# Gate/up blocks 2 to 9 of both FFNs by 7 products of halves instead of blocks 2, 3, 5, 6 and 7, with 3 of the 7 second weight parts made by adding transfers

## The chip, the core and the metric

One core of a Trainium2 chip runs the whole program. The metric is the device time of one execution in microseconds, the median of several runs.

## The reference, cut to what matters

A decoder layer on 512 rows of 1024 numbers: an FFN, a token mixer, a second FFN, each between norms. The change is in the two FFNs, which compute, with `w_gu` of 1024 x 5632 and `w_dn` of 2816 x 1024:

```python
def swiglu(h, w_gu, w_dn):
    g, u = jnp.split(h @ w_gu, 2, axis=-1)
    return (jax.nn.silu(g) * u) @ w_dn
...
        h = rmsnorm(x, g_pre[l, 0]) * (1 + sc1) + sh1
        x = x + 0.5 * gt1 * rmsnorm(swiglu(h, w_gu1[l], w_dn1[l]), g_post[l, 0])
```

Everything is float32 in and out.

## The kernel before

**Precision.** A float32 operand is used as two parts: `hi`, the value rounded for the matrix engine (made by ScalarE, ACT), and `lo`, the rest (made by VectorE, DVE, as the value minus `hi`). A product of two float32 tiles is three matmuls (`hi hi`, `hi lo`, `lo hi`), all accumulated in PSUM. `split` makes the two parts of a weight tile of 128 x 1024 numbers. Its outputs are called `whi` and `wlo`, and each of the two has `NW = 5` buffers; a weight as it comes from memory is called `raw`, and there are `NRAW = 4` buffers for it, 512 KB each.

**Gate/up.** The columns of `w_gu` are worked off in 11 blocks of 256 gate and 256 up columns. A plain block loads four `raw` tiles, splits them and runs 96 matmuls with 512 columns (four accumulators, 8 rows of tiles, 3 matmuls each; line 381). The blocks in `SEVEN` go through the function `seven` instead: the four `raw` tiles are taken as the four quarters a11, a12 (gate columns, upper and lower half of the contraction), a21, a22 (up columns) of a 2 x 2 matrix of blocks, and the output comes from 7 products of halves instead of 8. Seven weight combinations are needed: l11 = a11, l12 = a12, l22 = a22 as they are, and l1, l2, l3, l4, which are sums and differences, made by DVE in place in the `raw` tiles (4 instructions, lines 413 to 421). Each of the seven is split (7 ACT and 7 DVE instructions, lines 156 and 157), and each is the left side of 24 matmuls with 256 columns (line 429), in the order l11, l2, l1, l3, l12, l22, l4. Between the products DVE adds the partial results (`plus`, line 435, 5 instructions); the last of these, `gate2`, needs the whole block. Then ACT and DVE form silu(g) * u and split it for the down projection (lines 455 to 460).

**Order.** The instructions of each engine are in a fixed order, which a scheduler has laid down when the program was built; each engine works its own list off in order and waits at semaphores. SP issues the loads, also in a fixed order; a load waits until its buffer is free.

**Down projection.** `down` runs over two halves of the output columns (`dh`), and in each over 11 pairs of rows of `w_dn` (24 matmuls of 512 columns for a pair, line 193). In the first FFN, four pieces of the conditioning for the mixer (`mod_cols`: 2 MB of `w_ada`, 8 DVE multiply-adds, 8 small matmuls, line 269) are worked in beside plain gate/up blocks, at blocks 4, 8, 9 and 10. The residual rows (`xt`, 8 tiles) stay in SBUF through the FFN.

Of the kernel before, what the change touches and what calls it, by code (L numbers as in the profile page):

```python
# [8 lines left out]
F32 = mybir.dt.float32  # L9
F32R = mybir.dt.float32r  # L10
U8 = mybir.dt.uint8
BF16 = mybir.dt.bfloat16
AF = mybir.ActivationFunctionType
ALU = mybir.AluOpType

P = 128
T = 512
# [13 lines left out]
NW = 5  # L31
NMM = 6
LOOK = 4
SEVEN = (2, 3, 5, 6, 7)
KTAIL = 6
ROWS_A = (4, 5, 5, 4)

# [3 lines left out]
def tile_hybrid_layer(  # L41
# [17 lines left out]
    def nm(s):  # L59
        uid[0] += 1  # L60
        return f"{s}_{uid[0]}"
# [10 lines left out]
    def acc(shape=(P, 512)):  # L72
        return pm.tile(list(shape), F32, tag="mm", name=nm("mm"))
# [49 lines left out]
    def load_x(src, pin, between=()):  # L123
        for t in range(NT):
            xt[t] = [unit(), unit()]
            for h in range(2):
                i = nc.sync.dma_start(xt[t][h], src[t * P:(t + 1) * P, h * 512:(h + 1) * 512])
                if pin:
                    tc.keep_in_program_order(i)
                if between:  # L130
                    nc.sync.dma_start(*between.pop(0))
# [16 lines left out]
    def raw_load(src, shape):  # L148
        raw = sb.tile([P] + list(shape), F32, tag="raw", bufs=NRAW, name=nm("raw"))
        nc.sync.dma_start(raw, src)  # L150
        return raw

    def split(raw, shape, eng=None):
        hi = sb.tile([P] + list(shape), F32R, tag="whi", bufs=NW, name=nm("whi"))
        lo = sb.tile([P] + list(shape), F32R, tag="wlo", bufs=NW, name=nm("wlo"))
        nc.scalar.copy(hi, raw)  # L156
        (eng or nc.vector).tensor_tensor(lo, raw, hi.bitcast(F32), ALU.subtract)  # L157
        return hi, lo
# [32 lines left out]
    def mm3(ps, a, b, first, last):  # L191
        for n, (i, j) in enumerate(PARTS):
            nc.tensor.matmul(ps, a[i], b[j], start=first and n == 0, stop=last and n == 2)  # L193

    def cut(pair, cs):
        return pair[0][:, cs], pair[1][:, cs]
# [205 lines left out]
    def seven(w_gu, jb, hs, rs, act):  # L402

        gw, uw = gu_blocks(w_gu, jb)
        for b in (gw, uw):
            b.fetch()
        a11, a12, a21, a22 = gw.raw[0], gw.raw[4], uw.raw[0], uw.raw[4]
        t1, t2, t3, t4 = rs
        b11, b21, b22 = [lambda k, e, k0=k0, ts=ts: hs[k0 + k][e][:, ts] for k0, ts in
                         ((0, slice(0, 256)), (4, slice(0, 256)), (4, slice(256, 512)))]  # L410
        sh = (4, 256)
        l11 = split(a11, sh)
        nc.vector.tensor_tensor(a21, a21, a22, ALU.add)  # L413
        l1 = split(a21, sh)
        nc.vector.tensor_tensor(a21, a21, a11, ALU.subtract)
        l2 = split(a21, sh)
        l22 = split(a22, sh)
        nc.vector.tensor_tensor(a22, a22, a21, ALU.subtract)
        l3 = split(a22, sh)
        l12 = split(a12, sh)  # L420
        nc.vector.tensor_tensor(a12, a12, a21, ALU.subtract)
        l4 = split(a12, sh)
        x, y, z = [acc((P, 2, 256)) for _ in range(3)]

        def product(ps, left, right, first=False):
            for k in range(4):
                for j in range(2):
                    for n, (i, e) in enumerate(PARTS):
                        nc.tensor.matmul(ps[:, j], left[i][:, k, j * P:(j + 1) * P], right(k, e),  # L429
                                         start=first and k + j + n == 0, stop=k == 3 and n == 2,  # L430
                                         skip_group_check=True)

        def plus(ps, a, out=None):
            o = tmp((P, 2, 256)) if out is None else out
            nc.vector.tensor_tensor(o, ps, a, ALU.add)
            return o

        product(x, l11, b11, True)
        p1 = tmp((P, 2, 256))
        nc.scalar.copy(p1, x)  # L440
        product(y, l2, t2, True)
        u2 = plus(y, p1)
        product(z, l1, t1, True)
        product(y, l3, t3)
        u3 = plus(y, p1)
        up2 = plus(z, u3, u3)
        product(x, l12, b21)
        product(y, l22, t4)
        product(z, l4, b22)
        up1 = plus(y, p1, p1)  # L450
        gate2 = plus(z, u2, u2)
        a = [(unit(F32R), unit(F32R)) for _ in range(2)]
        for h, (g, u) in enumerate(((x, up1), (gate2, up2))):
            th = tmp((P, 2, 256))
            nc.scalar.activation(th, g, AF.Tanh, scale=0.5)
            nc.vector.scalar_tensor_tensor(th, th, 1.0, g, ALU.add, ALU.mult)
            nc.vector.scalar_tensor_tensor(th, th, 0.5, u, ALU.mult, ALU.mult)
            for j in range(2):
                ts = slice(h * 256, (h + 1) * 256)
                hilo(a[j][0][:, ts], a[j][1][:, ts], th[:, j])  # L460
        act.extend(a)

    def ffn(w_gu, w_dn, hs, extra, gate, after, ps=None, by_seven=(), keep=None):

        act = []
        rest = [b for b in range(KF // 2) if b not in by_seven][-len(extra):] if extra else []
        for jb in range(KF // 2):
            if by_seven and jb == 1:
                rs = right_sides(keep)
            if jb in by_seven:  # L470
                seven(w_gu, jb, hs, rs, act)
                continue
            if ps is None:
                gw, uw = gu_blocks(w_gu, jb)
                for kk in range(0, KD, 4):
                    gw.load(kk, kk + 4)
                    uw.load(kk, kk + 4)
                late = extra.pop(0)() if jb in rest else None
                ps = [[acc(), acc()] for _ in range(2)]
                for ts in (slice(0, 256), slice(256, 512)) if jb == 0 else (slice(0, 512),):  # L480
                    for kk in range(0, KD, 4):
                        gu_matmuls(ps, gw, uw, hs, range(kk, kk + 4), ts)
                if late:
                    late()
            for pg, pu in ps:
                th = tmp()
                nc.scalar.activation(th, pg, AF.Tanh, scale=0.5)
                nc.vector.scalar_tensor_tensor(th, th, 1.0, pg, ALU.add, ALU.mult)
                nc.vector.scalar_tensor_tensor(th, th, 0.5, pu, ALU.mult, ALU.mult)  # L489
                a = (unit(F32R), unit(F32R))  # L490
                hilo(a[0], a[1], th)
                act.append(a)
            ps = None
        down(w_dn, act, gate, after)

    def down(w, act, gate, after):
        nk = len(act)
        ss = [small(2, "ss", 4) for _ in range(NT)]
        yg = None
        g = []  # L500
        for dh in range(2):
            ys = [acc() for _ in range(NT)]
            groups = [(k, 2) for k in range(0, nk, 2)]
            if dh == 1:
                groups = groups[:-KTAIL // 2] + [(nk - KTAIL, KTAIL)]
            for k0, n in groups:
                wp = Block(w, k0, n, dh * 512, 512)
                wp.load()
                if dh == 0 and k0 in (0, 4):
                    gate(g, k0 // 4)  # L510
                for t in range(NT):
                    ts = slice(t * P, (t + 1) * P)
                    for k in range(n):
                        mm3(ys[t], cut(act[k0 + k], ts), wp[k], k0 + k == 0, k0 + k == nk - 1)
            if dh == 0:
                yg = [unit() for _ in range(NT)]
                post_first(ys, g[0], ss, yg)
            else:
                for t in range(NT):
                    post_second(t, ys[t], g[1], ss, yg)  # L520
                    after(t)
# [87 lines left out]

    with not_before(last):  # L610
        ffn(w_gu1[0], w_dn1[0], hs, extra, lambda g, h: mod_gate(g, 0, h, 0.5), after1, ps0, SEVEN,
            (1, lambda tp, k: xT[k][:, tp * 256:(tp + 1) * 256].unsqueeze(1)))
    hs = nxt[-1]


# [586 lines left out]
    load_x(xd, True)  # L1202

    h3 = {}

    def after2(t):
        if t == 0:
            nxt.append(h_tiles())
        if t % 2:
            make_h(t // 2, nxt[-1], sh3, sc3, h3)  # L1210

    down(w_out, mrg, lambda g, h: mod_gate(g, 1, h, 1.0), after2)


    def after3(t):
# [1 line left out]
            nc.sync.dma_start(out[t * P:(t + 1) * P, h * 512:(h + 1) * 512], xt[t][h])  # L1217

    ffn(w_gu2[0], w_dn2[0], nxt[-1], [], lambda g, h: mod_gate(g, 2, h, 0.5), after3,
        by_seven=SEVEN, keep=(2, lambda tp, k: h3[tp, k // 2]))  # L1220


# [26 lines left out]
```

## Time and profile before

| | |
|---|---|
| median of 3 runs | 1432.32 us (1431.89 to 1432.74) |
| the profiled execution | 1435.03 us, span in the profile 1433.3 us |
| PE (matmul) busy | 1375.0 us, 96% |
| DVE busy | 896.1 us, 63% |
| ACT busy | 577.7 us, 40% |
| POOL busy | 206.7 us, 14% |
| mean granted TensorE clock | 0.996 |

The profile is of one execution. PE is TensorE, DVE VectorE, ACT ScalarE, POOL GpSimd, and SP the engine that issues the loads; busy time is the union of an engine's instructions, and the span runs from the first to the last instruction. Stretches are given in us from the span's start. In the first FFN the gate/up blocks 2 to 10 run from 89.8 to 287 us and the down projection to 405 us; in the second FFN they run from 1108.4 to 1300.8 us, with the down projection behind them up to the end.

### The profile page before, as it was taken

The numbers are of one execution on the slowest core, as the hardware profiler recorded it, in microseconds if no ns is written. First come the engines' busy times: TensorE is split into PE (matmuls) and PEld (weight loads), VectorE is DVE, ScalarE is ACT, GpSimd is POOL, SyncE is SP. The second block draws the span as 40 slices with busy tenths as digits, with TensorE's granted clock in tenths as the row PEclk, the third lists the DMA queues.
The fourth block names the chain that finished last, engine by engine and source line by source line (L and its number), as shares of the span: only waits on it lengthen the run. The fifth ranks groups of instructions, "written<-read, shape, count | busy, mean of one in ns | idle before, by whom it ended". The sixth has DMA issues, their size and how long they took to land.

```text
span 1433.3 us, 18789 instructions
## 1 busy us (share of the span) xinstructions
PE 1375.0 (96%) x7197; PEld 1141.6 (80%) x7197; DVE 896.1 (63%) x1398; ACT 577.7 (40%) x999; POOL 206.7 (14%) x328
## 2 busy tenths in 40 slices
PE   4899999999999999999999999999999999999998
PEld 3699998878877877777888887788878989887886
DVE  6889797562266689762735546538577878637222
ACT  6444453232144476663723333333344434423221
POOL 5300000000051553440110202100050000000001
PEclk9999999999999999999999999999999999999999
DMA  9425237473235756322232232124611332436311
GB/s 323 141 67 165 86 111 226 146 243 98 88 121 165 232 156 176 90 67 88 88 111 81 59 87 61 59 74 140 228 59 60 103 105 87 147 88 196 127 59 59
DMA packets 160629, 174.49 MB, mean 122 GB/s; under 512 B 8842, under 2 KB 127734, under 8 KB 160540
## 3 DMA queue, kind: packets, MB, share of 16 engines
q1 hardware_dynamic: 160540, 173.31, 39.2%
q8 instruction: 56, 0.92, 0.3%
q14 instruction: 33, 0.27, 0.1%
HBM read 169.05 MB, written 4.23 MB: 121 GB/s over the span
## 4 chain that ended last, share of the span: by engine, by line
PE 73%; DVE 14%; DMA 4%; ACT 4%; issue 3%; POOL 1%; SPq 0%; DVEq 0%; ACTq 0%; POOLq 0%
PE mm L193 46%; PE mm L381 15%; PE mm L429 6%; DVE wlo L157 3%; ACT whi L156 2%; DMA raw<-in_w_gu_dram 2%; PE aux L1069 1%; DMA u<-in_w_ada_dram 1%; DVE u L200 1%; PE aux L880 1%; DVE u L868 1%; PE mm L891 1%; DVE t L214 1%; ACT u L864 1%; DVE raw L413 1%
## 5 line engine op out<-in xcount | busy, mean ns | idle before, releaser
L157 DVE TENSOR_TENSOR wlo<-raw,whi 128x1024 fp32r<-128x1024 f32 x248 | 307.9, 1249 | 293.0 <-ACT whi L156 284.0
L156 ACT CAST whi<-raw 128x1024 fp32r<-128x1024 f32 x250 | 259.5, 1050 | 482.1 <-PE mm L193 297.0
L193 PE MATMUL mm<-whi,u 128*128 128x512 f32 x1216 | 390.2, 397 | 1.5 <-ACT u L199 1.5
L193 PE MATMUL mm<-u,whi 128*128 128x512 f32 x896 | 289.5, 402 | 0.8 <-DVE u L1096 0.8
L193 PEld LDWEIGHTS mm<-whi,u 128*128 128x128 f32 x1216 | 228.2, 188 | 54.3 <-ACT u L199 1.7
L381 PE MATMUL mm<-u,whi 128*128 128x512 f32 (+1 forms) x832 | 249.6, 385 | 10.8 <-ACT u L199 9.7
L193 PE MATMUL mm<-wlo,u 128*128 128x512 f32 x608 | 240.4, 395 | 0.0
L429 PE MATMUL mm<-u,whi 128*128 128x256 f32 x1120 | 200.0, 281 | 2.4 <-ACT whi L156 2.1
L193 PEld LDWEIGHTS mm<-u,whi 128*128 128x128 f32 x896 | 167.0, 189 | 39.2 <-DVE u L1096 1.2
L381 PEld LDWEIGHTS mm<-u,whi 128*128 128x128 f32 x832 | 153.6, 190 | 46.5 <-ACT u L199 13.0
L193 PE MATMUL mm<-u,wlo 128*128 128x512 f32 x448 | 178.4, 399 | 0.0
L429 PEld LDWEIGHTS mm<-u,whi 128*128 128x128 f32 x1120 | 171.7, 188 | 4.0 <-ACT whi L156 3.2
L429 PE MATMUL mm<-u,wlo 128*128 128x256 f32 x560 | 157.1, 282 | 2.2 <-DVE wlo L157 2.2
L381 PE MATMUL mm<-u,wlo 128*128 128x512 f32 (+1 forms) x416 | 156.1, 382 | 0.0
L193 PEld LDWEIGHTS mm<-wlo,u 128*128 128x128 f32 x608 | 114.2, 188 | 27.8
L429 PEld LDWEIGHTS mm<-u,wlo 128*128 128x128 f32 x560 | 105.2, 188 | 3.3 <-DVE wlo L157 3.0
L193 PEld LDWEIGHTS mm<-u,wlo 128*128 128x128 f32 x448 | 84.7, 189 | 19.6
L308 POOL TENSOR_SCALAR sm<-ss 128x1 f32<-128x1 f32 x12 | 2.3, 192 | 651.4 <-ACT jk L315 651.4
L381 PEld LDWEIGHTS mm<-u,wlo 128*128 128x128 f32 x416 | 79.3, 191 | 16.2
L214 DVE SCALAR_TENSOR_TENSOR t<-raw,csil,t 128x512 f32<-128x512 f32 x98 | 74.2, 757 | 3.5 <-DMA raw<-in_w_ada_dram 1.4
L199 ACT CAST u<-t 128x256 fp32r<-128x256 f32 (+1 forms) x80 | 36.0, 469 | 75.5 <-DVE t L489 47.7
L837 POOL TENSOR_SCALAR u<-t,Ft 128x128 f32<-128x128 f32 (+1 forms) x64 | 41.9, 665 | 91.5 <-DMA t<-Fd 61.7
(201 smaller groups left out, 1384.8 us busy)
## 6 DMA issues: line engine op xcount, KB each, us to landing
raw<-in_w_gu_dram SPq DMA_DIRECT2D x88, 512.0 KB, 3.5
raw<-in_w_in_dram SPq DMA_DIRECT2D x64, 512.0 KB, 3.8
raw<-in_w_dn_dram SPq DMA_DIRECT2D x44, 512.0 KB, 3.9
raw<-in_w_ada_dram SPq DMA_DIRECT2D x64, 256.0 KB, 3.8
raw<-in_w_ada_dram SPq DMA_DIRECT2D x24, 512.0 KB, 4.7
u<-in_w_ada_dram SPq DMA_DIRECT2D x32, 256.0 KB, 6.4
raw<-in_w_in_dram SPq DMA_DIRECT2D x20, 256.0 KB, 2.9
t<-Fd SPq DMA_DIRECT2D x16, 256.0 KB, 5.1
```

Of the source, the lines that this page charges most:

```text
L156: nc.scalar.copy(hi, raw)
L157: (eng or nc.vector).tensor_tensor(lo, raw, hi.bitcast(F32), ALU.subtract)
L193: nc.tensor.matmul(ps, a[i], b[j], start=first and n == 0, stop=last and n == 2)
L199: nc.scalar.copy(hi, src)
L200: (eng or nc.vector).tensor_tensor(lo, src, hi.bitcast(F32), ALU.subtract)
L214: nc.vector.scalar_tensor_tensor(a, raw[:, j, :], csil[:, k:k + 1], a, ALU.mult, ALU.add)
L381: nc.tensor.matmul(p_[:, ts], w_[k][i][:, cs], hs[k][e][:, ts], start=ks[0] == 0 and n == 0, stop=ks[-1] == KD - 1 and n == 3 * len(ks) - 1)
L413: nc.vector.tensor_tensor(a21, a21, a22, ALU.add)
L429: nc.tensor.matmul(ps[:, j], left[i][:, k, j * P:(j + 1) * P], right(k, e), start=first and k + j + n == 0, stop=k == 3 and n == 2, skip_g ...
L837: nc.gpsimd.tensor_scalar(s_at(s, i), fb[:, 0:n], -1.0, Ft[:, i, h:h + 1], ALU.mult, ALU.add)
L864: nc.scalar.activation(s_at(S[e], i), s_at(S[e], i), AF.Exp, bias=nmx[e][:, i:i + 1], accum_out=rs[e][:, i:i + 1])
L868: nc.vector.tensor_scalar(s_at(S[e], i), s_at(S[e], i), rs[e][:, i:i + 1], None, ALU.mult)
```

## The change

`SEVEN` becomes all blocks from 2 to 9. In `seven` the combinations are made in another order and stand in other tiles, and three of the seven (l12, l22 and l4) are no longer split by DVE: ACT writes `hi` and then also the negative of the value, rounded, to `wlo`, and a transfer that POOL issues adds the value to it in place. The four pieces of the conditioning move: one to block 10, three into the first half of the down projection. The residual rows are no longer held through the FFN: they are loaded again (in the first FFN from the input, in the second from a copy `xe` in memory that is stored behind the mixer) at the start of the second half of the down projection.

```diff
-SEVEN = (2, 3, 5, 6, 7)
+SEVEN = tuple(range(2, 10))
...
+    def split_added(raw, shape):
+
+        hi = sb.tile([P] + list(shape), F32R, tag="whi", bufs=NW, name=nm("whi"))
+        lo = sb.tile([P] + list(shape), F32R, tag="wlo", bufs=NW, name=nm("wlo"))
+        nc.scalar.copy(hi, raw)
+        nc.scalar.activation(lo, raw, AF.Copy, scale=-1.0)
+        nc.gpsimd.dma_start(lo.bitcast(F32), raw, accum_op=ALU.add)
+        return hi, lo
...
+        nc.vector.tensor_tensor(a21, a21, a22, ALU.add)
         l11 = split(a11, sh)
-        nc.vector.tensor_tensor(a21, a21, a22, ALU.add)
+        nc.vector.tensor_tensor(a11, a21, a11, ALU.subtract)
+        l2 = split(a11, sh)
         l1 = split(a21, sh)
-        nc.vector.tensor_tensor(a21, a21, a11, ALU.subtract)
-        l2 = split(a21, sh)
-        l22 = split(a22, sh)
-        nc.vector.tensor_tensor(a22, a22, a21, ALU.subtract)
-        l3 = split(a22, sh)
-        l12 = split(a12, sh)
-        nc.vector.tensor_tensor(a12, a12, a21, ALU.subtract)
-        l4 = split(a12, sh)
+        nc.vector.tensor_tensor(a21, a22, a11, ALU.subtract)
+        l3 = split(a21, sh)
+        l12 = split_added(a12, sh)
+        l22 = split_added(a22, sh)
+        nc.vector.tensor_tensor(a11, a12, a11, ALU.subtract)
+        l4 = split_added(a11, sh)
...
-                late = extra.pop(0)() if jb in rest else None
+                late = extra.pop(0)() if extra and jb == KF // 2 - 1 else None
...
+            if dh == 1 and source is not None:
+                load_x(source, True)
...
+                late = extra.pop(0)() if extra and dh == 0 and k0 > 4 and k0 % 4 == 0 else None
...
+        for h in range(2):
+            nc.sync.dma_start(xe[t * P:(t + 1) * P, h * 512:(h + 1) * 512], xt[t][h])
```

Three places in the engines' lists show what the change makes of the order. All are of the first FFN, from block 6 to block 7; the second FFN reads alike.

The first is DVE at the end of block 6, before the change. `mm_317` and `mm_318` are accumulators of block 6, `raw_328` to `raw_331` are the tiles a11, a12, a21, a22 of block 7. L435 with `mm_318` at the sixth row is `gate2` of block 6, L415 makes l2 of block 7, and the last row is the second part of l2.

```order
L456 SCALAR_TENSOR_TENSOR t2_326_1889<-t2_326_1889,mm_316_1705 128x512
L413 TENSOR_TENSOR raw_330_1909<-raw_330_1909,raw_331_1911 128x1024
L435 TENSOR_TENSOR t2_319_1732<-mm_317_1706,t2_319_1732 128x512
L457 SCALAR_TENSOR_TENSOR t2_326_1889<-t2_326_1889,t2_319_1732 128x512
L157 TENSOR_TENSOR wlo_335_1919<-raw_330_1909,whi_334_1918 128x1024
L435 TENSOR_TENSOR t2_320_1758<-mm_318_1707,t2_320_1758 128x512
L200 TENSOR_TENSOR u_323_1886<-t2_326_1889,u_322_1885 128x256
L415 TENSOR_TENSOR raw_330_1909<-raw_330_1909,raw_328_1905 128x1024
L200 TENSOR_TENSOR u_325_1888<-t2_326_1889,u_324_1887 128x256
L456 SCALAR_TENSOR_TENSOR t2_327_1897<-t2_327_1897,t2_320_1758 128x512
L457 SCALAR_TENSOR_TENSOR t2_327_1897<-t2_327_1897,t2_321_1808 128x512
L157 TENSOR_TENSOR wlo_337_1924<-raw_330_1909,whi_336_1923 128x1024
```

The same place on DVE after the change. `raw_330` to `raw_333` are now a11, a12, a21, a22 of block 7; L444 with `mm_320` is `gate2` of block 6, L423 makes l2 of block 7, and the last row is L426, which makes l3.

```order
L421 TENSOR_TENSOR raw_332_1995<-raw_332_1995,raw_333_1997 128x1024
L209 TENSOR_TENSOR u_325_1972<-t2_328_1975,u_324_1971 128x256
L444 TENSOR_TENSOR t2_322_1844<-mm_320_1793,t2_322_1844 128x512
L209 TENSOR_TENSOR u_327_1974<-t2_328_1975,u_326_1973 128x256
L423 TENSOR_TENSOR raw_330_1991<-raw_332_1995,raw_330_1991 128x1024
L465 SCALAR_TENSOR_TENSOR t2_329_1983<-t2_329_1983,t2_322_1844 128x512
L466 SCALAR_TENSOR_TENSOR t2_329_1983<-t2_329_1983,t2_323_1894 128x512
L166 TENSOR_TENSOR wlo_337_2006<-raw_330_1991,whi_336_2005 128x1024
L209 TENSOR_TENSOR u_325_1972<-t2_329_1983,u_324_1971 128x256
L209 TENSOR_TENSOR u_327_1974<-t2_329_1983,u_326_1973 128x256
L166 TENSOR_TENSOR wlo_339_2010<-raw_332_1995,whi_338_2009 128x1024
L426 TENSOR_TENSOR raw_332_1995<-raw_333_1997,raw_330_1991 128x1024
```

In both lists `gate2` of block 6 stands ahead of the instruction that makes l2 of block 7; the second parts of l12, l22 and l4 are gone from DVE.

The second place is ACT in block 7 after the change: the first part of l3 (`whi_340`), then both parts of l12, l22 and l4 (`whi_342` to `wlo_347`), then l11 of block 8 (`whi_364`).

```order
L449 COPY t2_351_2061<-mm_348_2034 128x512
L165 CAST whi_340_2014<-raw_332_1995 128x1024
L157 CAST whi_342_2018<-raw_331_1993 128x1024
L158 ACTIVATE wlo_343_2019<-raw_331_1993 128x1024
L157 CAST whi_344_2023<-raw_333_1997 128x1024
L158 ACTIVATE wlo_345_2024<-raw_333_1997 128x1024
L157 CAST whi_346_2029<-raw_330_1991 128x1024
L158 ACTIVATE wlo_347_2030<-raw_330_1991 128x1024
L165 CAST whi_364_2243<-raw_360_2234 128x1024
```

Each `whi` and `wlo` of l12, l22 and l4 stands behind the first part of l3, which itself reads what L426 wrote.

The third place is SP's list of loads after the change, with the waits: DMASW is the landing of an adding transfer, DMAHW that of a load. The rows are the tiles of blocks 6, 7 and the first of block 8.

```order
L150 DMA raw_301_1750<-in_w_gu1_dram 128x4x256 [waits DMAHW1_49,DMASW1_49,Activation_49]
L150 DMA raw_302_1752<-in_w_gu1_dram 128x4x256 [waits DMAHW3_49,DMAHW6_49,DMASW2_49,Activation_49]
L150 DMA raw_303_1754<-in_w_gu1_dram 128x4x256 [waits DMASW3_49,Activation_49]
L150 DMA raw_330_1991<-in_w_gu1_dram 128x4x256 [waits DMAHW0_49,DVE_49]
L150 DMA raw_331_1993<-in_w_gu1_dram 128x4x256 [waits DMAHW5_49,DMASW4_49,Activation_49]
L150 DMA raw_332_1995<-in_w_gu1_dram 128x4x256 [waits DMAHW2_49,DMAHW7_49,DMASW5_49,Activation_49]
L150 DMA raw_333_1997<-in_w_gu1_dram 128x4x256 [waits DMASW6_49,Activation_49]
L150 DMA raw_360_2234<-in_w_gu1_dram 128x4x256 [waits DMAHW4_49,DVE_49]
```

The loads of a12, a21 and a22 of a block wait for the landing of the first, second and third adding transfer of the block ahead; before the change none of a block's four loads waited for a transfer of that kind.

## Rows read from the trace of the kernel before

**Rows 1.** The page: busy time and share of the span by engine.
```profile
PE 1375.0 (96%) x7197; PEld 1141.6 (80%) x7197; DVE 896.1 (63%) x1398; ACT 577.7 (40%) x999; POOL 206.7 (14%) x328
```
**Rows 2.** Chain of waits, in order of time: start us, length us, what.
```profile
131.11 22.48 PE mm L381 x96
154.38 31.45 PE mm L429 x264
...
307.93 97.08 PE mm L193 x416
...
1321.59 105.47 PE mm L193 x452
```
**Rows 3.** Busy time by window, second FFN: three blocks by seven, one plain.
```profile
1171.92:1192.00 20.08, 20.08 (x173) 20.08 (x172) 16.58 (x19) 8.79 (x11) 0.00 (x0) 1.00 0.29 89
...
1213.00:1233.30 20.30, 19.83 (x166) 19.35 (x164) 19.48 (x24) 11.74 (x16) 0.00 (x0) 1.00 0.46 140
1233.40:1255.80 22.40, 22.40 (x98) 17.99 (x97) 11.36 (x17) 7.88 (x13) 0.00 (x0) 1.00 0.40 131
```
**Rows 4.** Busy time by window: blocks 2 to 9 of each FFN.
```profile
89.76:263.60 173.84, 171.07 (x1153) 156.90 (x1152) 143.12 (x186) 70.65 (x97) 0.00 (x0) 1.00 0.45 140
1108.36:1278.10 169.74, 167.92 (x1129) 153.31 (x1128) 123.75 (x151) 69.97 (x94) 0.00 (x0) 1.00 0.34 106
```
**Rows 5.** Timeline of DVE, first FFN, from block 6 to 7.
```profile
195.49 0.68 DVE L435 TENSOR_TENSOR t<-mm,t 128x512 f32<-128x512 f32 x1
196.09 0.42 DVE L200 TENSOR_TENSOR u<-t,u 128x256 fp32r<-128x256 f32 x1
196.43 1.22 DVE L415 TENSOR_TENSOR raw<-raw,raw 128x1024 f32<-128x1024 f32 x1
197.56 0.42 DVE L200 TENSOR_TENSOR u<-t,u 128x256 fp32r<-128x256 f32 x1
...
204.63 2.36 DVE L157 TENSOR_TENSOR wlo<-raw,whi 128x1024 fp32r<-128x1024 f32 x2 [0.34 <-ACT whi L156]
```
**Rows 6.** Timeline of ACT, the same place.
```profile
196.21 0.63 ACT L455 ACTIVATE t<-t 128x512 f32<-128x512 f32 x1 [1.02 <-DVE t L435]
197.74 2.00 ACT L156 CAST whi<-raw 128x1024 fp32r<-128x1024 f32 x2 [0.89 <-DVE raw L415]
...
200.25 0.58 ACT L440 COPY t<-mm 128x512 f32<-128x512 f32 x1
203.55 2.00 ACT L156 CAST whi<-raw 128x1024 fp32r<-128x1024 f32 x2 [2.72 <-DVE raw L418]
```
**Rows 7.** Timeline of PE, the same place: end of product l11, start of l2.
```profile
196.93 0.28 PE L429 MATMUL mm<-u,wlo 128*128 128x256 f32 x1
198.83 0.74 PE L429 MATMUL mm<-u,whi 128*128 128x256 f32 x4 [1.62 <-ACT whi L156]
```
**Rows 8.** The page, queues: packets, MB, share of 16 engines.
```profile
q1 hardware_dynamic: 160540, 173.31, 39.2%
```
**Rows 9.** The page, DMA issues: KB each, median us from issue to landing.
```profile
raw<-in_w_gu_dram SPq DMA_DIRECT2D x88, 512.0 KB, 3.5
...
raw<-in_w_ada_dram SPq DMA_DIRECT2D x64, 256.0 KB, 3.8
raw<-in_w_ada_dram SPq DMA_DIRECT2D x24, 512.0 KB, 4.7
```
**Rows 10.** DMA from 184 to 206 us: GB/s in 40 slices.
```profile
GB/s 197 357 352 19 30 95 251 357 235 65 149 367 354 34 0 0 0 0 0 0 0 0 0 0 0 0 24 141 339 376 73 0 0 0 0 0 0 0 30 0
```
**Rows 11.** The page, groups: busy us, mean ns, idle us before.
```profile
L157 DVE TENSOR_TENSOR wlo<-raw,whi 128x1024 fp32r<-128x1024 f32 x248 | 307.9, 1249 | 293.0 <-ACT whi L156 284.0
L156 ACT CAST whi<-raw 128x1024 fp32r<-128x1024 f32 x250 | 259.5, 1050 | 482.1 <-PE mm L193 297.0
...
L214 DVE SCALAR_TENSOR_TENSOR t<-raw,csil,t 128x512 f32<-128x512 f32 x98 | 74.2, 757 | 3.5 <-DMA raw<-in_w_ada_dram 1.4
```
**Rows 12.** Timeline of PE, first FFN, first half of the down projection.
```profile
304.10 0.39 PE L193 MATMUL mm<-whi,u 128*128 128x512 f32 x1
306.26 0.50 PE L295 MATMUL aux<-pair,ones 128*128 128x512 f32 x1 [1.77 <-ACT pair L199]
```

More of the change, by code (lines that the diff above doesn't have):

```diff
@@ L461, in seven, with ffn @@
         act.extend(a)
-    def ffn(w_gu, w_dn, hs, extra, gate, after, ps=None, by_seven=(), keep=None):
+    def ffn(w_gu, w_dn, hs, extra, gate, after, ps=None, by_seven=(), keep=None,
+            source=None):
         act = []
-        rest = [b for b in range(KF // 2) if b not in by_seven][-len(extra):] if extra else []
         for jb in range(KF // 2):
@@ L493, in ffn, with down @@
             ps = None
-        down(w_dn, act, gate, after)
-    def down(w, act, gate, after):
+        down(w_dn, act, gate, after, source, extra)
+    def down(w, act, gate, after, source=None, extra=()):
         nk = len(act)
@@ L514, in down @@
                         mm3(ys[t], cut(act[k0 + k], ts), wp[k], k0 + k == 0, k0 + k == nk - 1)
+                if late:
+                    late()
             if dh == 0:
@@ L611, in tile_hybrid_layer @@
         ffn(w_gu1[0], w_dn1[0], hs, extra, lambda g, h: mod_gate(g, 0, h, 0.5), after1, ps0, SEVEN,
-            (1, lambda tp, k: xT[k][:, tp * 256:(tp + 1) * 256].unsqueeze(1)))
+            (1, lambda tp, k: xT[k][:, tp * 256:(tp + 1) * 256].unsqueeze(1)), x)
     hs = nxt[-1]
@@ L1204, in tile_hybrid_layer @@
     h3 = {}
+    xe = dr.tile([T, D], F32, name="xe")
     def after2(t):
@@ L1219, in tile_hybrid_layer @@
     ffn(w_gu2[0], w_dn2[0], nxt[-1], [], lambda g, h: mod_gate(g, 2, h, 0.5), after3,
-        by_seven=SEVEN, keep=(2, lambda tp, k: h3[tp, k // 2]))
+        by_seven=SEVEN, keep=(2, lambda tp, k: h3[tp, k // 2]), source=xe)
 _INS = ['x', 'c', 'w_ada', 'b_ada', 'g_pre', 'g_post', 'w_gu1', 'w_dn1', 'w_gu2', 'w_dn2',
```

## The prediction

> **What bounds the kernel now.** I read the page first: PE is busy 96% of the span, DVE 63%, ACT 40% [rows 1]. The chain of waits then shows what that is made of: unbroken runs of matmuls, 97.08 us of the first down projection and 105.47 us of the second among them [rows 2]. So whatever the change takes off PE counts in full, if PE is fed. The chain also gives the pace: 96 matmuls of a plain block take 22.48 us, and 264 matmuls of 256 columns 31.45 us, 0.119 us each; a block by seven has 168 of them, 20.0 us. A block that PE works without waiting is thus 2.5 us cheaper by seven.
>
> The windows show the other side. In the three blocks by seven of the second FFN, DVE is busy 16.58 of 20.08 us in the first and 19.48 of 20.30 us in the third; in the plain block behind them 11.36 of 22.40 us [rows 3]. DVE is nearly the bound where such blocks follow one another, and the plain blocks let it catch up. Blocks 2 to 9 take 173.84 us in the first FFN and 169.74 us in the second [rows 4]. In the first, three pieces of the conditioning are in it, whose small matmuls take the 0.79 us between the end of the plain block (131.11 + 22.48 = 153.59) and the next run at 154.38 [rows 2]; they move, so what the change works on is 173.84 - 2.37 + 169.74 = 341.2 us.
>
> The timelines of block 7 of the first FFN show where such a block waits. DVE makes `gate2` of block 6 at 195.49, then the difference for l2 of block 7 at 196.43 [rows 5]; ACT rounds it from 197.74 [rows 6]; PE has ended l11 at 197.05 and goes on at 198.83 [rows 7]. From the difference to ACT it is 1.31 us, from ACT to PE 1.09 us.
>
> **The change, step by step: the block by seven.** By count it is a gain: 8 blocks at 20.0 us are 160 us. But the order puts a chain into each block. Let s be the moment at which PE starts a block; its predecessor's last matmul ends about 0.2 us later, and DVE's `gate2` starts at s + 0.3. From starts in rows: `gate2` takes 0.60, a half `lo` 0.34, a big instruction 1.13 us (196.43 to 197.56), the wait of DVE for ACT's rounding is 1.08 (203.55 to 204.63) [rows 5, 6]; ACT's big ones follow at 0.96 us (two in 2.00, the last of 1.05) [rows 6, 11].
> - l2: the difference starts at s + 1.25, ACT at 2.56, the second part at 3.65 on DVE, and is there at 4.9. PE ends l11 at 24 x 0.119 = 2.9 and waits 2.0 us.
> - l3: DVE goes on with two half `lo` (4.78, 5.12), l1 (5.46) and the sum for l3 (6.59); ACT rounds that at 7.9. DVE's second part of l3 comes behind `plus` for l2, at 9.55, so PE starts l3 near 10.8 instead of 10.6 and ends it at 13.7.
> - l12: ACT's two passes stand behind l3's rounding: 8.86 and 9.82, end 10.9. Then POOL issues, and the transfer lands A later. PE starts l12 at 10.9 + A, and three products of 2.86 us follow: the block takes **19.5 + A**.
> - The tiles close the same circle. ACT ends both parts of l4 at 14.7; the transfer lands at 14.7 + A; only then is the buffer of the next a22 free, whose load takes 3.5 us [rows 9]; the sum a21 + a22 (1.13) and a half `lo` (0.34) stand ahead of `gate2` in DVE's list. That is 19.7 + A, against `gate2` at 0.3 of the next block: 19.4 + A.
>
> The ACT pass with the factor -1 has no row; an ACTIVATE and a COPY of the same 512 columns take 0.63 and 0.58 us [rows 6], so I take that of the rounding. Both circles are free of the wait for PE's other products, so the sum stands if A is over 2.8 us; below that the waits for l2 and l3 alone leave 22.3 us.
>
> **What A is.** No transfer in this trace is issued by POOL or adds: all but instruction fetches are of SP's queue [rows 8]. Lower bound: a load of 512 KB lands after 3.5 us [rows 9]. Upper bound: twice the 512 KB row that takes longest, 2 x 4.7 = 9.4 us, since the adding transfer has to read its target as well as its source [rows 9]. The nearest row is the load, and a second reading of 512 KB at the 357 GB/s that the queue reaches [rows 10] is 1.5 us: 5.0. POOL's issue is in no row; I take A = **6.0**, a little under the middle of the bounds. A block then takes 25.5 us.
>
> The page DMA: Bandwidth & Descriptors of the Trainium skill (Anatomy of one DMA, SWDGE path) gives a transfer issued by POOL 2.0 us and its bytes at 436 GB/s, which would be 3.2 us for 512 KB; it says nothing of adding. By that figure a block would take 22.7 us and the program 1452 us, an estimate from that page. No run here shows a transfer of that kind so far.
>
> **Sum.** The first block by seven (2) is prepared while block 1 still runs, and its transfers land before PE comes to them: 20.0 us. Blocks 3 to 9 take 25.5 each: 178.5. Both FFNs: 2 x 198.5 = 397.0, against 341.2: +55.8 us.
> - Three conditioning pieces in the down projection: each is 8 instructions of 0.757 us on DVE [rows 11] over two groups of rows (48 matmuls at 0.234 us, 11.2 us), beside two splits of 1.13: 8.3 of 11.2 us. The loads are six of 512 KB in that time, 280 GB/s, under the 357 seen [rows 10]. With such loads for the gate PE waits 2.16 us there once (304.10 to 306.26) [rows 12]. Between nothing and 10 us; I take 3.
> - Residual rows: 8 loads of 256 KB in each FFN and 8 stores in one, 2.1 MB each, some 6 us at 357 GB/s; they stand among the loads of the down projection, whose second half is one unbroken run on PE [rows 2], and are hidden by its 50 us. Were that cover gone, 6 us an FFN. I take nothing.
> - Holding fewer tiles shortens nothing by itself: no row shows a wait for them.
>
> In all +59 us. The profiled execution was 1435.03 us, its span 1433.3 and 1.7 around it, 2.7 over the median of 1432.32; 1435.0 + 58.8 - 2.7 = **1491 us**.
>
> **Rivals.**
> 1. *The transfer is as quick as a load* (A = 3.5 to 4.5). For it: the load's row. Against: it reads twice as much and POOL issues it. A block takes 23.0 us, blocks 2 to 9 of both FFNs 2 x (20.0 + 161) = 362: +21 us, with 3 in the down projection 1456 us at A = 3.5.
> 2. *The transfer is slow or is issued late* (A over 7.5). For it: three of them within 4 us of ACT's time, beside loads on the same queue engines, and the 9.4 us bound. At 9.4: 28.9 us a block, 2 x (20.0 + 202.3) = 444.6, +103, with 10 in the down projection 1546 us. One way to it: an issue on POOL that must wait until an instruction of DVE ends, 1.22 us [rows 5], is 14 x 1.2 = 17 us more than the forecast, 1508 us. SBUF — State Buffer of the Trainium skill (section SBUF: two separate sides, the box on SWDGE) describes this: POOL can't write descriptors while DVE holds the port that they share. It names DVE's two-port modes for it, and holds two-input instructions, which nearly all here are, for harmless; no run here shows either.
> 3. *Faster: DVE was the limit, and is relieved.* Without three passes of 1.13 us DVE's 19.48 us [rows 3] become 16.1, and all eight blocks run at PE's 20.0 us: 320 against 341.2, with the 3 us of the down projection 1414 us. It is decided by the time of a block: below (341.2 - 40) / 14 = 21.5 us the change pays. Against: the wait for l2 follows from `gate2` standing ahead of it, as block 7 shows, and alone leaves 22 us.
> 4. *No change*: a block near 21.5 us, of chance only.
>
> **How the numbers follow.** A difference of 0.2%, 3 us, is about what a measurement of this kernel can tell. Forecast (A 4.5 to 7.5, 1470 to 1512 us): 0.55. Rival 1: 0.18. Rival 2: 0.17. Rival 3: 0.07. Rival 4: 0.03. Faster 0.07, same 0.03, slower 0.90. The range takes in rival 1 and half of rival 2: 1450 to 1530 us, which leaves out some 0.18.
>
> **What will show it.** Right: in blocks 3 to 9 of both FFNs PE waits twice in each block, some 2 us ahead of l2, put down to ACT or DVE, and some 3 us ahead of l12, put down to the transfer; a block takes 23 to 28 us; the load of a22 is issued right after the third transfer lands; DVE's busy share in these stretches falls under 0.75. The time from the end of ACT's pass to PE's first matmul with that `wlo` is A. Wrong: blocks at 20 to 21 us; or PE waiting for something else, such as the loads of a11 or PSUM; or more than 10 us lost in the down projections.

## The result and the profile after

The changed kernel takes **1543.81 us** (median of 4 runs, 1541.79 to 1548.49) against 1432.11 us before (1431.38 to 1432.74): ratio **1.0785**, 95% interval 1.0757 to 1.0812. That is 111.7 us slower. I had forecast 1491 us with a range up to 1530: the sign and one of the two circles that I forecast came true, the size did not.

The page of the changed kernel, the lines that answer to [rows 1, 8, 9], with the shares of the chain by engine and by line between them:

```profile
PE 1408.0 (91%) x7629; PEld 1189.3 (77%) x7629; DVE 910.4 (59%) x1434; ACT 643.5 (42%) x1083; POOL 247.8 (16%) x376
...
q1 hardware_dynamic: 163996, 179.60, 37.1%
q0 software_dynamic: 6912, 25.17, 8.9%
...
PE 59%; DVE 14%; DMA 14%; ACT 8%; issue 4%; POOL 1%; SPq 0%; DVEq 0%; POOLq 0%; ACTq 0%
PE mm L202 42%; DMA wlo<-raw 8%; PE mm L390 7%; PE mm L438 4%; DMA raw<-in_w_gu_dram 4%; DVE wlo L166 2%; ACT wlo L158 2%; ACT whi L157 2%; ACT whi L165 1%; PE aux L1084 1%; DVE u L209 1%; DVE raw L421 1%; DVE raw L423 1%; DVE t L223 1%; ACT u L879 1%
...
L159 POOL DMA_DIRECT2D wlo<-raw x48 | 41.2, 859 | 460.6 <-ACT wlo L158 331.2
...
raw<-in_w_gu_dram SPq DMA_DIRECT2D x88, 512.0 KB, 5.1
...
wlo<-raw POOLq DMA_DIRECT2D x48, 512.0 KB, 7.4
```

The 48 adding transfers, called transfers from here on, have a queue of their own (q0). One lands 7.4 us after its issue (median), and the loads of `w_gu` beside them take 5.1 us instead of 3.5. In the chain of what ended last, 14% is now DMA, 8% the transfers and 4% the loads of `w_gu`.

Busy time by window, as in [rows 4] and [rows 3]: blocks 2 to 9 of each FFN with their sum, and two blocks of the first FFN from one sum a21 + a22 to the next (us; busy time and count of PE, weight loads, DVE, ACT, POOL; granted clock, DMA share, GB/s):

```profile
88.38:317.02 228.64, 186.93 (x1346) 178.63 (x1345) 127.55 (x163) 101.36 (x134) 20.53 (x24) 0.91 0.52 129
1163.42:1388.59 225.17, 184.46 (x1346) 177.00 (x1345) 124.71 (x158) 99.79 (x131) 20.69 (x24) 0.91 0.54 132
sum 453.81, PE 371.39 PEld 355.63 DVE 252.25 ACT 201.15 POOL 41.22; mean PE 185.70 PEld 177.82 DVE 126.13 ACT 100.57 POOL 20.61
...
199.90:229.70 29.80, 25.83 (x192) 24.35 (x192) 16.72 (x22) 13.54 (x19) 2.54 (x3) 0.94 0.51 126
229.70:259.40 29.70, 24.49 (x175) 23.50 (x174) 16.77 (x21) 12.82 (x17) 2.55 (x3) 0.89 0.51 124
```

All of the loss is in these two stretches: 453.8 us instead of 341.2, +112.6, while the rest of the span fell from 1433.3 - 341.2 = 1092.1 to 1543.5 - 453.8 = 1089.7. A block takes 29.7 us, and DVE is busy in 16.8 of them.

Which of the two circles sets that pace stands in the chain of waits, one turn of it (start us, length us, what):

```profile
229.72 1.23 DVE raw L421
...
231.28 0.60 DVE t L444
...
232.21 1.14 DVE raw L423
...
236.53 1.14 DVE wlo L166
...
237.69 1.24 DVE raw L426
...
238.95 1.05 ACT whi L165
240.00 0.95 ACT whi L157
240.95 0.95 ACT wlo L158
...
244.74 0.97 ACT wlo L158
245.71 0.29 issue
246.00 8.45 DMA wlo<-raw
...
254.51 4.84 DMA raw<-in_w_gu_dram
...
259.47 1.23 DVE raw L421
```

This is the tile circle, and PE (here in no row of the chain) is not in it: the sum (L421), the differences for l2 and l3, ACT's six passes for l12, l22 and l4, the **third** transfer (8.45 us), the load of the next a22 (4.84 us), the next sum. One turn is 259.47 - 229.72 = 29.75 us. The three transfers of this block took 5.6, 7.4 and 8.4 us from issue to landing, each longer than the one ahead. POOL issues them 1.9 us apart (242.21, 244.10, 246.00), 0.3 us after ACT has made each `wlo`, but they land 3.8 and 2.9 us apart: they stand in line.

The records of single packets show what the third one waits for. In order, 144 of q0's 6912 packets belong to each transfer. The third's issue ends at 246.85, and its first packet starts at 251.04; in the time between, the queues' packets took these shares of the 16 DMA engines:

```profile
q0 software_dynamic: 162, 0.56, 67.5%
q1 hardware_dynamic: 515, 0.51, 35.2%
```

So the engines are full: 2.8 of these 4.2 us are packets of the two transfers ahead, and 1.5 us are packets of a load. The third's own packets run for 3.0 us after that.

### The profile page after: what moved, and what is told of

Same layout as the page of the kernel before. It is cut to its first block, busy times and chain, and to the rows that moved or that the text cites. A ratio compares the mean times of both kernels' runs of the same rounds, so it can differ in the third digit from the quotient of the medians.

```text
span 1543.5 us, 20027 instructions
## 1 busy us (share of the span) xinstructions
PE 1408.0 (91%) x7629; PEld 1189.3 (77%) x7629; DVE 910.4 (59%) x1434; ACT 643.5 (42%) x1083; POOL 247.8 (16%) x376
## 3 DMA queue, kind: packets, MB, share of 16 engines
q0 software_dynamic: 6912, 25.17, 8.9%
## 4 chain that ended last, share of the span: by engine, by line
PE 59%; DVE 14%; DMA 14%; ACT 8%; issue 4%; POOL 1%; SPq 0%; DVEq 0%; POOLq 0%; ACTq 0%
PE mm L202 42%; DMA wlo<-raw 8%; PE mm L390 7%; PE mm L438 4%; DMA raw<-in_w_gu_dram 4%; DVE wlo L166 2%; ACT wlo L158 2%; ACT whi L157 2%; ACT whi L165 1%; PE aux L1084 1%; DVE u L209 1%; DVE raw L421 1%; DVE raw L423 1%; DVE t L223 1%; ACT u L879 1%
## 5 line engine op out<-in xcount | busy, mean ns | idle before, releaser
L166 DVE TENSOR_TENSOR wlo<-raw,whi 128x1024 fp32r<-128x1024 f32 x218 | 272.6, 1253 | 272.8 <-ACT whi L165 258.6
L165 ACT CAST whi<-raw 128x1024 fp32r<-128x1024 f32 x220 | 228.6, 1048 | 465.0 <-PE mm L202 272.0
L438 PE MATMUL mm<-u,whi 128*128 128x256 f32 x1792 | 356.2, 300 | 57.0 <-ACT whi L165 44.5
L438 PEld LDWEIGHTS mm<-u,whi 128*128 128x128 f32 x1792 | 302.0, 207 | 65.0 <-ACT whi L165 50.3
L438 PE MATMUL mm<-u,wlo 128*128 128x256 f32 x896 | 269.2, 303 | 25.4 <-DMA wlo<-raw 22.5
L202 PEld LDWEIGHTS mm<-u,whi 128*128 128x128 f32 x896 | 167.5, 190 | 39.1 <-DVE u L1111 1.2
L390 PE MATMUL mm<-u,whi 128*128 128x512 f32 (+1 forms) x448 | 128.1, 375 | 11.3 <-ACT u L208 8.8
L159 POOL DMA_DIRECT2D wlo<-raw x48 | 41.2, 859 | 460.6 <-ACT wlo L158 331.2
L444 DVE TENSOR_TENSOR t<-mm,t 128x512 f32<-128x512 f32 x80 | 55.1, 689 | 95.7 <-PE mm L438 94.1
L390 PEld LDWEIGHTS mm<-u,whi 128*128 128x128 f32 x448 | 81.7, 193 | 29.4 <-ACT u L208 13.3
L202 PEld LDWEIGHTS mm<-u,wlo 128*128 128x128 f32 x448 | 85.0, 190 | 19.4
L390 PE MATMUL mm<-u,wlo 128*128 128x512 f32 (+1 forms) x224 | 80.2, 370 | 0.0
```

The lines of the kernel that those rows point to most:

```text
L159: nc.gpsimd.dma_start(lo.bitcast(F32), raw, accum_op=ALU.add)
L390: nc.tensor.matmul(p_[:, ts], w_[k][i][:, cs], hs[k][e][:, ts], start=ks[0] == 0 and n == 0, stop=ks[-1] == KD - 1 and n == 3 * len(ks) - 1)
```

## The experiments

All times below are medians; where the text gives no interval, the kernel ran once. "Blocks" is blocks 2 to 9 of both FFNs together, from the windows of the profiled execution; before it was 341.2.

| run | edit to the changed kernel | time, us | blocks, us |
|---|---|---|---|
| (the change) | | 1543.8 | 453.8 |
| e4_dve | no transfers, DVE makes all second parts | 1440.6 | 353.3 |
| e1_raw6 | six raw tiles | 1502.4 | 411.7 |
| e2_plain | transfers copy, the addition is left out | 1497.1 | 404.5 |
| e3_l12 | only l12 by a transfer | 1510.5 | 418.4 |
| e8_l4_four | only l4 by a transfer | 1514.8 | 423.4 |
| e9_l4_eight | only l4 by a transfer, eight raw tiles | 1435.5 | 340.9 |
| e10_raw8 | eight raw tiles | 1482.0 | 391.5 |
| e5_early | eight raw tiles, next block's first parts earlier in the code | 1479.6 | 389.8 |
| x8_ahead | no transfers, next block's first parts earlier in the code | 1443.5 | 354.6 |
| e7_oldorder | no transfers, old order of the differences | 1447.0 | 355.6 |
| x10_pool1 | no transfers, l4's second part by GpSimd | 1447.2 | 357.4 |
| e6_rows | only the rows and the conditioning (five blocks by seven) | 1431.8 | |

**Without the transfers (e4_dve).**

```diff
-        l12 = split_added(a12, sh)
-        l22 = split_added(a22, sh)
+        l12 = split(a12, sh)
+        l22 = split(a22, sh)
...
-        l4 = split_added(a11, sh)
+        l4 = split(a11, sh)
```

> No transfer: all seven second parts by DVE, in the changed order of the combinations, blocks 2 to 9, residual rows reloaded, conditioning moved. Theory that the transfers are the whole loss and the waits for l2 and l3 stay: 22.3 us a block, 2 x (20 + 7 x 22.3) = 352 against 341, with 3 in the down projection 1446 us. Rival 1 (eight blocks in a row are the loss, as DVE can't keep up): over 1480 us. Rival 2 (a block runs at the 20.5 us of the blocks by seven of before): 1424 us.

Measured 1440.6 us, ratio to before 1.0055 (1.0039 to 1.0071). Theory and measurement are 5 us apart. The three transfers, with the three passes on ACT that go with them, thus cost 103 of the 112 us; no run has the passes without the transfers. What is left is a block with one wait, 21.7 to 22.1 us from one such wait to the next in the first FFN and 23.1 once; PE's row with one of them (start, length, what, idle before and its releaser):

```profile
228.70 0.40 PE L438 MATMUL mm<-u,wlo 128*128 128x256 f32 x1 [1.53 <-DVE wlo L166]
```

**The other half alone (e6_rows)**: the old `seven` and its five blocks, with the residual rows out and the conditioning in the down projection.

> The other half of the change alone: residual rows out and back and the conditioning's reads in the down projection, with blocks 2, 3, 5, 6 and 7 by seven as before, no transfers and the old order of the differences. Theory: it costs nothing to speak of, 1430 to 1436 us. Rival: the rows' reloads hold the last down projection, or the conditioning holds the first, 1440 us or more.

Measured 1431.83 us, ratio 0.9998 (0.9988 to 1.0009): it costs nothing.

**The tile circle (e1_raw6).** `NRAW` 4 to 6, `NU` 69 to 65 to make room.

> Six raw buffers instead of four (and 65 unit tiles instead of 69 to make room), all else as in the changed kernel. The load of a block's a22 then waits for the first adding transfer of the block ahead, not for the third. Theory of the tiles (the block's 29.5 us are the circle third transfer landed, load of a22, sum a21 + a22, and so on to the third transfer): the circle opens, a block takes what PE needs behind its waits for the three transfers, 10.9 + 0.3 for ACT and the issue, 12.0 to the third landing (three transfers of 3.7 us one behind the other), 2.9 for the last product: 26.1 us, the program 1544 - 14 x 3.4 = 1496 us, and the wait for l2 falls to 2 us. Rival (PE's own wait for the transfers sets the block, the tiles only follow): blocks stay at 29.5 us, 1544 us.

Measured 1502.4 us, 41 less and 6 over what the theory gave: the tile circle set the pace, and another wait stands at some 26 us a block (411.7 / 16 = 25.7 in the mean; 26.8 in the first FFN and 24.7 in the second).

**The addition (e2_plain).** The transfers copy `raw` over `wlo`, and the addition is left out.

```diff
-        nc.gpsimd.dma_start(lo.bitcast(F32), raw, accum_op=ALU.add)
+        nc.gpsimd.dma_start(lo.bitcast(F32), raw)
```

> The three transfers copy instead of adding (the addition is left out, so the second parts of l12, l22 and l4 are the whole values). Theory that the adding makes a transfer slow: a packet of 4 KB takes near 0.2 us instead of 0.33, a transfer holds the queue some 2.2 us instead of 3.7, the third lands 5.5 us after its issue instead of 8.3, blocks of 26.7 us, 1505 us. Rival (the way by POOL's queue is slow, whatever is done with the bytes): landing times and 1544 us unchanged within 5.

Measured 1497.1 us, 8 under the theory. From the page of this run, the queue of the transfers and two rows of the DMA issues:

```profile
q0 software_dynamic: 6912, 25.17, 4.5%
...
raw<-in_w_gu_dram SPq DMA_DIRECT2D x88, 512.0 KB, 4.5
...
wlo<-raw POOLq DMA_DIRECT2D x48, 512.0 KB, 4.7
```

The same 6912 packets take 4.5% of 16 engines' span instead of 8.9%: 16 x 1495.2 x 0.045 / 6912 = 0.156 us for a packet on average, and with the addition 16 x 1543.5 x 0.089 / 6912 = 0.318 us. The addition doubles the time of a packet, moves the median landing from 4.7 to 7.4 us and costs 47 us.

**One transfer at a time (e3_l12, e8_l4_four, e9_l4_eight).** First the one that PE needs earliest, l12's; l22 and l4 go back to DVE.

> Only l12 goes by an adding transfer; l22 and l4 are split by ACT and DVE as the others. Theory that three transfers stand in line: one alone lands 5.1 us after its issue, a block takes 10.9 + 0.3 + 5.1 + 8.6 = 24.9 us, 1544 - 14 x 4.6 = 1480 us. Rival (a transfer issued by POOL costs the same whether it is alone or not): landing of 7.4 us, 27 us a block, 1509 us.

Measured 1510.5 us: the expectation was 30 us short, and even my rival price was passed by a little. One transfer of three costs 70 of the 103 us. The chain of waits shows a circle through PE (one turn; the 70 matmuls are the rest of l12, then l22 and l4):

```profile
203.59 6.53 DMA wlo<-raw
...
210.16 10.91 PE mm L438 x70
...
226.60 1.15 DVE raw L426
...
229.67 1.05 ACT wlo L158
...
231.02 6.54 DMA wlo<-raw
```

A turn is 231.02 - 203.59 = 27.43 us. This is the first circle of my prediction, "19.5 + A"; here it reads 20.6 + 6.8, with A from ACT's end at 230.72 to the transfer's landing at 231.02 + 6.54 = 237.56. The 70 matmuls took 10.91 us, where 0.119 us each would make 8.3; the granted clock over them was 0.76, and the last section tells more. A single transfer, with none ahead of it, is over the 6.0 of the forecast too.

Then the one that PE needs last, l4's, with four and with eight raw tiles. The pair is meant to separate what a transfer costs by itself from what waits for it. With eight tiles (`NRAW` 8, `NU` 61) no load has to wait for a transfer of the block just ahead.

```diff
-        l12 = split_added(a12, sh)
-        l22 = split_added(a22, sh)
+        l12 = split(a12, sh)
+        l22 = split(a22, sh)
```

> Only l4's second part by an adding transfer (l12's and l22's on DVE), four raw tiles as in the change. Theory: the transfer reads a11's tile, in whose place the next block's a22 is loaded, so the tile circle stays with one transfer in it: some 15.5 us from the sum to ACT's end, 6.5 us to the landing, 4 to 5 us of load make 26 to 27 us a block, 1500 to 1520 us. Rival (a transfer is dear only where PE waits for it, and l4 is PE's last product, which leaves it 9 us more than l12): about the 1440.6 us of the kernel without transfers, 1435 to 1455 us.

> The same with eight raw tiles, so that a load waits for a transfer two blocks back, which has long landed. Theory (waits alone make the transfer dear): nothing is left that waits for it but l4's product, the last of the block, and the sum of the next block can go on: blocks of 20.5 to 22.5 us, 1425 to 1450 us. Rival (an adding transfer costs by itself, in the queue and in the clock): within 15 us of the run with four tiles, 1490 us or more.

Measured **1514.8 us with four tiles, 1435.5 us with eight** (ratio of the latter to before 1.0025, 1.0015 to 1.0035), both as the theory had it. With four tiles, two blocks by window:

```profile
190.10:217.00 26.90, 22.40 (x169) 21.53 (x169) 18.62 (x23) 10.94 (x15) 0.83 (x1) 0.94 0.36 98
217.00:244.60 27.60, 23.19 (x170) 22.40 (x169) 18.62 (x23) 10.95 (x15) 0.85 (x1) 0.88 0.37 96
```

and in its timeline of DVE the sum a21 + a22:

```profile
218.14 1.23 DVE L421 TENSOR_TENSOR raw<-raw,raw 128x1024 f32<-128x1024 f32 x1 [6.01 <-DMA raw<-in_w_gu_dram]
```

With eight tiles, two blocks by window, and the two FFNs:

```profile
197.20:217.20 20.00, 20.00 (x171) 19.91 (x170) 18.09 (x23) 10.61 (x15) 0.85 (x1) 1.00 0.47 132
217.20:236.90 19.70, 19.70 (x171) 19.70 (x169) 17.01 (x20) 11.38 (x15) 0.83 (x1) 1.00 0.49 134
...
88.49:259.80 171.31, 162.68 (x1346) 161.76 (x1345) 146.43 (x182) 87.47 (x121) 6.96 (x8) 0.98 0.47 132
1109.77:1279.40 169.63, 162.60 (x1346) 161.49 (x1345) 143.47 (x180) 86.11 (x119) 6.92 (x8) 0.98 0.47 133
```

Against e4_dve, the kernel without transfers, the same transfer makes 74 us more with four tiles and 5 us less with eight. e4_dve has four tiles, and no run has eight without transfers: how much of the 5 us is the tiles' is not shown. With four tiles DVE stands still for 6.01 us until the load behind the transfer has landed; with eight the two blocks shown run at PE's 20.0 and 19.7 us. Not all do: in the first FFN the sum still waits 4.40 us at 127.21 and 3.40 at 150.79, each time for a load issued right after a transfer had landed, and PE waits 3.61 us at 140.18 and 2.57 at 164.50. The scheduler also lays the lists out differently for eight tiles (the next sum comes earlier on DVE), so the run changes that with the tiles. The transfer's own time differs as well: from issue to landing it is 8.9 us with four tiles (median; 4.9 to 9.9) and 4.9 with eight (4.7 to 7.8). No transfer is ahead of it in either. For the one with four tiles issued at 206.09 the packets show what holds it: between the end of the issue, 206.92, and its first packet, 210.41, only loads have packets:

```profile
q1 hardware_dynamic: 698, 0.70, 74.5%
```

The one with eight tiles issued at 207.91 has its first packet 1.44 us later and lands after 4.81 us. So the pair does not separate fully: with four tiles the transfer is itself longer, as loads are in flight beside it.

**All three transfers with eight tiles (e10_raw8, e5_early).**

> The whole change with eight raw tiles instead of four and nothing else. Theory: the tile circle is gone, and the second circle, PE's, is left: the transfer for l12, the gate that needs this product, the next sum behind the gate on DVE; 25.5 to 27 us a block, 1490 to 1510 us, as with six tiles (1502.4). Rival: with six tiles a load still waited for the first transfer of the block ahead, and that made the 1502; with eight 1440 to 1475 us.

> The three adding transfers as they are, but nothing of the next block has to stand behind them: eight raw tiles instead of four (so no load waits for a transfer of the block ahead), and the sum, the first difference and the splits of l11 and l2 of the next block are issued ahead of this block's additions out of PSUM. Theory (the transfers are dear only by what waits for them: the load of a22 behind the third landing, and the next block's sum behind the gate that needs the product with l12): blocks near PE's 20 us plus 0 to 2 us of lost clock, 1420 to 1450 us. Rival (the adding transfers themselves, three of 512 KB each block on one queue and the slower clock beside them, set the pace): no block under 26 us, 1490 us or more.

Measured 1482.0 and 1479.6 us: both between theory and rival, and as good as one kernel, since the scheduler put the sum at the same place in either. The trace of e10_raw8 shows why the eight tiles don't settle it for three transfers. Two rows of DVE:

```profile
159.03 1.23 DVE L421 TENSOR_TENSOR raw<-raw,raw 128x1024 f32<-128x1024 f32 x1 [3.23 <-DMA raw<-in_w_gu_dram]
...
162.51 1.22 DVE L426 TENSOR_TENSOR raw<-raw,raw 128x1024 f32<-128x1024 f32 x1
```

The sum of a later block now stands ahead of the difference for l3 of the block at work (L426), and it still waits for a load that stands behind a transfer, that of the block two before it: the third transfer, issued at 146.42, lands at 153.94, the load is issued at 154.01, and the sum starts at 159.03. So it is again a load behind a transfer, reached by another way; this is read from the trace, no run shows it apart.

**Three attempts at a faster kernel.**

> No transfers: eight blocks by seven, all second parts on DVE, and the sum, the first difference and the splits of l11 and l2 of the next block issued ahead of this block's last additions. Theory: what kept the same kernel without this order at 21.9 us a block was 1.7 us of wait for the first parts, behind the last additions of the block ahead on DVE; without it a block takes PE's 20.0 to 20.4 us, 16 blocks by 1.5 to 1.9 us less than 1440.6 gives 1411 to 1417 us. Rival: DVE, busy 18.5 us of each block, is late elsewhere in it (ahead of l12 or l4), and the time stays at 1430 to 1440 us.

Measured 1443.5 us, ratio 1.0087 (1.0069 to 1.0105). That is neither theory nor rival. The edit moved the code but not the order: in DVE's timeline the sum still stands behind the additions out of PSUM. And I had put e4_dve's wait at the wrong place: by its trace it is for a second part made by DVE, some 70 matmuls into the block, not for the first parts at its start.

> Eight blocks by seven with the old order of the differences, all second parts on DVE, the rest of the change in: what the new order of the differences is worth by itself, against 1440.6 us with the new order. Theory: the order matters little where DVE makes every part, 1435 to 1446 us. Rival: the old order's longer chain of differences costs a further 1 to 2 us in each of 16 blocks, 1456 to 1472 us.

Measured 1447.0 us in one run, 1 us over the theory's range. That is 6 us over the median of e4_dve but 3 over its profiled execution (1444.0), and the blocks differ by 2.3 us: the order matters little, and one run can't tell how much.

> No transfers: eight blocks by seven, l4's second part by GpSimd's own subtraction, the other six on DVE. GpSimd's one subtraction of this shape took 2.6 us before, against DVE's 1.2. Theory: it is off the path (l4 is PE's last product), and DVE's 1.2 us a block come off the wait ahead of each block: 20.5 to 21.9 us a block, 1420 to 1440 us. Rival: GpSimd and DVE slow each other and the wait grows: 1445 us or more.

Measured 1447.2 us, ratio 1.0115 (1.0090 to 1.0139): the rival's time, but not its reason: GpSimd's subtraction took 3.4 us (median; 2.6 was the figure of before), while PE's wait ahead of a `wlo` of DVE stayed at 1.5 us. Where the 4 us in the blocks go was not followed up. No version beat the kernel before.

## Why the prediction was wrong, step by step

- **PE's pace and the count of matmuls**: right. Where nothing waits, a block by seven takes 20.0 and 19.7 us (e9_l4_eight).
- **The tile circle**: right in its form, "19.4 + A". From the sum to the end of ACT's last pass I had 15.9 us (from s - 1.2 to s + 14.7); the chain shows 245.71 - 229.72 = 15.99. It also ended as said: the load of a22 is issued at 254.51, right after the third transfer lands.
- **The failed step: "A = 6.0, a little under the middle of the bounds"**, one number for all three transfers. For the first of the block it is right: 0.3 us from ACT to POOL and 5.6 to land are 5.9 us. For the third, on which the tile circle rests, it is 0.29 + 8.45 = 8.74 us, since packets of the two others and of a load go first. The load behind it takes 4.96 us up to the sum, not 3.5. That is +2.7 and +1.5 us: 25.5 + 4.2 = 29.7, as measured. Over 14 blocks it is 59 us, and blocks 2 to 9 took 453.8 - 397.0 = 56.8 us more than the sum. Rival 2 named this very thing ("three of them within 4 us of ACT's time, beside loads") and was given 0.17; the forecast treated the circles as equal and so missed that the tile circle alone carries the third landing.
- **The sub-way of rival 2**, POOL's issue held by an instruction of DVE: no sign of it. The issue took 0.832 to 1.044 us in all 48 cases, and the one at 242.21 ran beside a DVE instruction that lasted from 241.74 to 242.96. SBUF — State Buffer of the Trainium skill (section Who interferes with whom) says that a probe saw a copy on DVE stall a transfer of POOL, but not a two-input `tensor_tensor`; the trace agrees for the latter, as the instruction at 241.74 is of that kind.
- **The figure of the page** DMA: Bandwidth & Descriptors of the Trainium skill (Anatomy of one DMA, SWDGE path), 3.2 us for 512 KB: for an adding transfer the trace doesn't bear it out, none of the 48 landed before 4.5 us, and the median is 7.4. Plain copies of POOL (e2_plain) took 2.8 us at the fastest and 4.7 in the median, in line and beside loads; none of the runs has one by itself.
- **Waits on PE**: both are there in the block shown, in another size. Ahead of l2 it is 3.16 us at 234.53, not 2.0, because the sum now waits for its tile; ahead of l12's second part 0.72 us for the transfer at 247.82 and 0.88 for DVE's addition just before, not 3.2, because PE itself is late by then.
- **Down projection +3 us, residual rows 0**: the rest of the span fell by 2.4 us, and e6_rows ran at 0.9998 of before. The 3 us were not needed. The 2.16 us of PE's wait there were read from start to start; the row itself has 1.77 [rows 12].
- **DVE relieved** (rival 3): its share fell to 16.8 of 29.7 us, but it was idle for want of a tile, not free to speed PE up. That rival's condition was a block under 21.5 us, with 20.0 for the first. No run is clearly under it: e9_l4_eight, the best, stands at it, (340.9 - 40) / 14 = 21.5, and its time is that of before within 0.4%.

How much of the third transfer's 8.45 us is the line can be read from the packets of the block shown. Its first packet starts 5.04 us after the issue, against 1.44 for an undisturbed transfer (e9_l4_eight, landing after 4.81). Of the 3.6 us more, about 1.5 are the load's packets and the rest, some 2.1, those of the transfers ahead. What decides which queue's packets go first stays open: in e8_l4_four the loads alone held a single transfer back.

## What to carry to other kernels

A transfer's time counts in full where something stands behind its landing, and as far as e9_l4_eight shows hardly where nothing does: ask which tile the transfer reads, which load takes that tile's place, and what waits for that load. The same transfer stood for 74 us here with four tiles, and with eight the kernel with it was within 0.3% of before; and where the circle was closed, halving the time of a packet took off 47 us. Where several transfers are issued within a few microseconds, price the last one in the line, in a circle that ends with it, and price the loads beside it with it.

## What the runs showed of the hardware

The granted clock was the new thing here. It was 1.00 in these stretches before [rows 4] and is 0.91 now. The rows around one wait of PE show where it goes (windows as above):

```profile
231.40:234.90 3.50, 0.37 (x2) 0.30 (x2) 3.46 (x6) 2.10 (x3) 0.00 (x0) 1.00 0.00 0
235.00:238.40 3.40, 2.96 (x14) 2.92 (x14) 3.37 (x5) 1.52 (x4) 0.00 (x0) 0.50 0.00 0
238.50:245.80 7.30, 7.30 (x60) 6.95 (x58) 3.38 (x4) 6.75 (x7) 1.70 (x2) 1.00 0.34 57
```

After a wait of 3.16 us TensorE works for 3.4 us at 0.50, the lower level of 1.2 GHz, and runs 14 matmuls in 2.96 us where 60 take 7.30 us at 1.00: 0.21 us each instead of 0.12. So a wait of PE here costs more than its length. In the changed kernel that lies beside the tile circle, which doesn't go through PE; in e3_l12, whose circle does, it is in the 10.91 us for 70 matmuls, 2.6 us a turn. In e4_dve, with one wait of 1.5 us a block, the clock was 1.00 and 0.99 over the blocks of the two FFNs.

An adding transfer's packets take twice as long as those of a copy, 0.318 against 0.156 us, and POOL's issue of one takes 0.859 us on average. How soon a transfer's packets start depends on what else is in flight: 1.44 us after the issue where little else was (e9_l4_eight, at 207.91), 4.32 us beside loads (e8_l4_four, at 206.09), 5.04 us behind two transfers and a load (the changed kernel, at 246.00).
